# A limit of 8 blocks on how far ahead weight halves are split

## The chip, the cores and the metric

The kernel runs on one core of a Trainium2 chip. The metric is the device time of one execution in microseconds (us), the median of several runs. TensorE (PE) multiplies matrices, VectorE (DVE) and ScalarE (ACT) work element by element, GpSimd (POOL) likewise, and the queue of SyncE (SPq) issues the transfers of weights from HBM. Each of these works through its own instructions in the order in which the program lists them.

## The reference

Two decoder layers in float32 for 256 tokens of width 1024:

```python
# layer 0: attention (8 stick-breaking heads, 8 latent heads), then a dense SwiGLU, hidden width 3584
h = _attention_layer(h, ...)
h = x + (silu(xn @ w_gate) * (xn @ w_up)) @ w_down
# layer 1: a state-space layer with GLU, then a SwiGLU with 8 experts, two for each token
h = _s5_layer(h, ...)
logits = xt @ w_router
top_vals, top_idx = lax.top_k(logits, 2)
gates = softmax(top_vals)
out[t] = sum over the two experts e of t: gate * ((silu(xt @ w_gate[e]) * (xt @ w_up[e])) @ w_down[e])
```

The expert stage reads all 8 experts, each with three matrices of 1024 x 3584, and is the larger part of the kernel's time.

## The kernel before

All weights pass through one stream of blocks, which `all_blocks` lists in the order of use. A block is 128 partitions by 2048 float32, 1 MB (1.0486 million bytes). `fetch` issues the transfer of the next block of the stream on SPq whenever a raw buffer is free in the program's order (`fill`, `drop`), and counts it in `nload`. Five raw buffers exist from the start; others come in as the earlier layers give up memory (`ex`, `ey`, `we0`, `tm`, `rot`, `wy0`, the pair `gx0`/`gx1`, `xl`, a pair from the ring of split halves, `sa`), so in the expert stage there are 15.

A product in float32 is made from three products in a faster format: a value w is split into wh and wl = w - wh, and `mm3` multiplies wh with the other side's high and low parts, and wl with its high part. Weights are split half a block at a time by `half`: ScalarE copies the half to wh (L228) and VectorE subtracts to get wl (L229). After the second half of a block its raw buffer is given back, and the next transfer of the stream is issued for it; that transfer waits until the split has read the buffer. The split halves stand in a ring, of six pairs first and five in the expert stage.

`take` hands out the next split half. Before that it splits halves ahead, up to `self.ahead` of them beyond the one in use (5, and 4 in the expert stage), as long as their blocks have been issued:

```python
while len(self.pairs) < min(i + ahead + 1, self.nsplit) and self.loaded:
    self.half()
```

The expert stage works on chunks (e, f): expert e, and 512 of the 3584 hidden columns. A chunk has four blocks of gate and up weights and two of down weights. Experts 0, 2, 4 and 6 in this order are wide (128 token places, split weights, three products each); experts 1, 3, 5 and 7 are narrow (64 places): their weights are multiplied as they come, in float32, and are not split. Their raw blocks lie in a list of their own (`whole`) and are given back when their products are done. `count` orders the experts by how many tokens they have, so that those with more become wide.

`MIXED` is the order of the chunks. It begins with three or four wide chunks, then alternates narrow and wide ones, and ends each pair of experts with narrow chunks alone. For experts 2 and 3, and the start of expert 4:

```
(2,0) (2,1) (2,2) (3,0) (2,3) (3,1) (2,4) (3,2) (2,5) (3,3) (2,6) (3,4) (3,5) (3,6) (4,0) ...
```

`ffn` runs the chunks in this order, and the down product of a chunk comes after the gate and up products of the next one; `ffn_order` lists the blocks accordingly, four of gate and up, then the two of down of the chunk before. So the down blocks of (2,6) stand behind the gate and up blocks of (3,4), and after them come 12 narrow blocks before those of (4,0). With experts 0 and 1 it is 18 narrow blocks between the down blocks of (0,6) and the first of (2,0).

When a wide expert's last down product is done, its rows are scaled into Y on ScalarE (L1672) and VectorE (L1673), in two halves n = 0 and 1, each as soon as its part is done and the one before it is used. The products that put Y back in the order of tokens (`scatter`, L1681 and L1682) are listed within the following narrow chunks (`hook`, `step`), and so is the gathering of the next wide expert's tokens (`prep`, L1620). L724 and L758 are the narrow chunks' products, L257 to L259 those of `mm3`; L742 turns a narrow chunk's hidden values, L1727 the selection of a wide expert's tokens.

Of the kernel before, what the change touches and what calls it, by code (L numbers as in the profile page):

```python
# [147 lines left out]
class Net:  # L148
# [19 lines left out]
    def plan(self, blocks):  # L168


        self.blocks, self.nload, self.loaded, self.plain, self.pairs, self.used = blocks, 0, [], {}, [], 0
        self.whole = []
        self.nsplit = 2 * sum(not isinstance(b, tuple) or len(b) == 3 for b in blocks)
        self.fill()

    def fetch(self, buf, keep=True):


        if self.nload == len(self.blocks):
            if keep:  # L180
                self.free.append(buf)
            return
        src = self.blocks[self.nload]
        self.nload += 1
        src, *how = src if isinstance(src, tuple) else (src,)
        src = src() if callable(src) else src
        n = src.shape[-1]
        if isinstance(buf[0], tuple):
            w = [p.tile([P, 1024], F32, tag=t, name="raw")[:, :n // 2] for p, t in buf]
            for x in range(2):  # L190
                self.nc.sync.dma_start(w[x], src[:, n // 2 * x:n // 2 * (x + 1)])
        else:
            w = buf[0].tile([P, 2048], F32, tag=buf[1], name="raw")[:, :n]
            self.nc.sync.dma_start(w, src)
            if len(how) != 1:
                w = [w[:, :n // 2], w[:, n // 2:]]
        if how == [None]:
            w = w if isinstance(w, list) else [w[:, :n // 2], w[:, n // 2:]]
            self.whole.append(([a[:, 512 * x:512 * x + 512] for a in w for x in range(2)], buf if keep else None))
        elif len(how) == 1:  # L200
            self.plain[how[0]] = (w, buf if keep else None)
        else:
            self.loaded.append((w, buf if keep else None, how))

    def fill(self):
        while self.free and self.nload < len(self.blocks):
# [6 lines left out]

    def half(self, sub=None):

        ws, buf, gain = self.loaded[0]
        x = self.second
        w = ws[x]
        pr = self.ring.pop(0)
        self.ring.append(pr)  # L220
        wh, wl = (pool.tile([P, 1024], F32R, tag=tag, name="w" + nm)[:, :w.shape[-1]] for (pool, tag), nm in zip(pr, "hl"))
        if gain:
            for j in range(2):
                c, g = slice(512 * j, 512 * j + 512), self.gain(gain[0], gain[1] + j + 2 * x)
                self.nc.scalar.activation(wh[:, c], w[:, c], AF.Copy, scale=g)
                self.nc.vector.scalar_tensor_tensor(out=wl[:, c], in0=w[:, c], scalar=g, in1=wh[:, c].bitcast(F32), op0=ALU.mult, op1=ALU.subtract)
        else:
            self.nc.scalar.copy(wh, w)  # L228
            (sub or self.sub).tensor_tensor(out=wl, in0=w, in1=wh.bitcast(F32), op=ALU.subtract)  # L229
        self.pairs.append((wh, wl))  # L230
        self.second ^= 1
        if x:
            self.loaded.pop(0)
            self.drop(buf)
# [5 lines left out]
    def take(self, kk, ahead=None):  # L240


        i = self.used
        ahead = self.ahead if ahead is None else ahead
        while len(self.pairs) < min(i + ahead + 1, self.nsplit) and self.loaded:
            self.half()
        self.used += 1
        n = self.pairs[i][0].shape[-1] // kk
        return [tuple(t[:, j * n:j * n + n] for t in self.pairs[i]) for j in range(kk)]
# [118 lines left out]
    def attention(self, kp):  # L368
# [4 lines left out]
        with ExitStack() as st:  # L373
# [266 lines left out]
            def out(n, half):  # L640
                W = self.takek(4, 0)
                for b in range(2):
                    if half == 0:
                        pw[n, b] = bank([P, 512])
                    for kk in range(4):
                        k = 4 * half + kk
                        self.mm3(pw[n, b], mh[:, k, blk[b]], ml[:, k, blk[b]], *W[kk], k == 0, k == KD - 1)
# [1180 lines left out]
```

## Time and profile before

| | us |
|---|---|
| median of 3 runs | 1317.21 (1316.95 to 1317.34) |
| the profiled execution | 1316.26 |
| its span, first to last instruction | 1313.3 |
| TensorE busy | 1271.5 (97%) |
| VectorE busy | 831.7 (63%) |
| ScalarE busy | 635.8 (48%) |
| transfers, mean over the span | 321 GB/s |

The profile names a group of instructions by the line of the kernel, the engine, the operation and the tiles it writes and reads. Busy time of TensorE is modelled: products are pipelined, each is shown with its whole latency, so that busy is not the same as working at peak rate. An idle time ahead of an instruction is shown in brackets with what ended it. In the tables of windows each row gives the window, its length, the busy time of PE, PEld (weight loads), DVE, ACT and POOL with the number of instructions, then the granted clock of TensorE as a share of full speed, the busy share of the 16 DMA engines, and GB/s.

### The profile page before, as it was taken

The page shows a single profiled execution, that of the slowest core. Times are in us where ns is not written, and L with a number is a line of the kernel's source. Part 1 is how long each engine was busy: PE and PEld are TensorE (multiplying, and loading weights), DVE is VectorE, ACT ScalarE, POOL GpSimd, SP SyncE. Part 2 cuts the span into 40 slices and gives each one's busy share as a digit, 9 for nine tenths or more (in the row PEclk, how much of TensorE's full clock was granted, in tenths as well). Part 3 has the DMA queues.
Part 4 walks back from the last instruction along what each step waited for, and adds up shares of the span by engine and source line. Part 5 has one row for each costly group of instructions (what it writes and reads, how often), then busy time and mean ns, then how long its engine had stood idle before and what let it go on. Part 6 is the DMA issues. An engine that isn't in the chain of part 4 may idle for free.

```text
span 1313.3 us, 18300 instructions
## 1 busy us (share of the span) xinstructions
PE 1271.5 (97%) x6782; PEld 905.1 (69%) x6782; DVE 831.7 (63%) x1114; ACT 635.8 (48%) x833; POOL 177.9 (14%) x284
## 2 busy tenths in 40 slices
PE   8999999999998999999999999799999989999997
PEld 8867999999997777664567665457655645756652
DVE  6877868567876897652377565248755525855642
ACT  6665444444444676551366554236644425645530
POOL 2842993013611000000000000000000000000000
PEclk9999999999999899999999999899999989999999
DMA  8505654545437699999999999999999999899991
GB/s 315 214 1 199 235 191 140 211 167 189 166 128 300 226 349 364 419 418 418 418 417 417 420 418 418 381 415 375 384 419 417 418 373 420 336 405 416 419 418 72
DMA packets 66368, 421.21 MB, mean 321 GB/s; under 512 B 7504, under 2 KB 8784, under 8 KB 21472
## 3 DMA queue, kind: packets, MB, share of 16 engines
q1 hardware_dynamic: 65088, 418.15, 80.4%
q10 hardware_dynamic: 1008, 1.27, 0.3%
q8 instruction: 55, 0.90, 0.3%
q0 software_dynamic: 176, 0.56, 0.1%
q14 instruction: 41, 0.34, 0.1%
HBM read 418.89 MB, written 1.05 MB: 320 GB/s over the span
## 4 chain that ended last, share of the span: by engine, by line


## 5 line engine op out<-in xcount | busy, mean ns | idle before, releaser
L229 DVE TENSOR_TENSOR wl<-raw,wh 128x1024 fp32r<-128x1024 f32 (+1 forms) x456 | 549.3, 1236 | 155.7 <-ACT wh L228 139.1
L228 ACT CAST wh<-raw 128x1024 fp32r<-128x1024 f32 (+1 forms) x456 | 468.3, 1045 | 187.2 <-PE dn L259 57.9
L724 PE MATMUL pgu<-raw,we 128*64 128x512 f32 x896 | 203.7, 596 | 0.0
L257 PE MATMUL pgu<-wh,wy 128*128 128x512 f32 x448 | 178.2, 398 | 0.0
L258 PE MATMUL pgu<-wl,wy 128*128 128x512 f32 x448 | 174.7, 390 | 0.8 <-DVE wl L229 0.8
L259 PE MATMUL pgu<-wh,wy 128*128 128x512 f32 x448 | 174.5, 390 | 0.0
L724 PEld LDWEIGHTS pgu<-raw,we 128*64 128x64 f32 x896 | 61.1, 137 | 115.4 <-issue 113.4
L257 PE MATMUL pgu<-dxh,wh 128*128 128x256 f32 x448 | 127.3, 284 | 0.5 <-DVE h L686 0.5
L259 PE MATMUL pgu<-dxh,wl 128*128 128x256 f32 x448 | 126.8, 283 | 0.0
L258 PE MATMUL pgu<-dxl,wh 128*128 128x256 f32 x448 | 126.7, 283 | 0.0
L257 PE MATMUL dn<-wh,gh 128*128 128x512 f32 x280 | 112.0, 400 | 0.0
L258 PE MATMUL dn<-wl,gh 128*128 128x512 f32 x280 | 109.4, 391 | 0.0
L259 PE MATMUL dn<-wh,gl 128*128 128x512 f32 x280 | 109.3, 390 | 0.0
L758 PE MATMUL dn<-raw,gh 128*64 128x512 f32 x448 | 101.9, 597 | 0.5 <-ACT gh L744 0.5
L257 PEld LDWEIGHTS pgu<-wh,wy 128*128 128x128 f32 x448 | 84.1, 188 | 22.6 <-issue 4.1
L259 PEld LDWEIGHTS pgu<-wh,wy 128*128 128x128 f32 x448 | 84.1, 188 | 17.9
L258 PEld LDWEIGHTS pgu<-wl,wy 128*128 128x128 f32 x448 | 84.2, 188 | 17.5 <-DVE wl L229 1.2
L797 DVE TENSOR_TENSOR gl<-pgt,gh 128x512 fp32r<-128x512 f32 x27 | 18.7, 692 | 114.3 <-ACT gh L796 113.4
L257 PEld LDWEIGHTS pgu<-dxh,wh 128*128 128x128 f32 x448 | 85.9, 192 | 1.1 <-DVE h L686 0.7
L258 PEld LDWEIGHTS pgu<-dxl,wh 128*128 128x128 f32 x448 | 86.0, 192 | 0.3
L259 PEld LDWEIGHTS pgu<-dxh,wl 128*128 128x128 f32 x448 | 85.9, 192 | 0.0
L796 ACT CAST gh<-pgt 128x512 fp32r<-128x512 f32 x27 | 15.8, 585 | 143.3 <-PE pgt L790 143.3
(445 smaller groups left out, 1566.0 us busy)
## 6 DMA issues: line engine op xcount, KB each, us to landing
raw<-in_wm_dram SPq DMA_DIRECT2D x292, 1024.0 KB, 10.3
raw<-in_wm_dram SPq DMA_DIRECT2D x88, 512.0 KB, 10.6
raw<-in_wd_dram SPq DMA_DIRECT2D x42, 1024.0 KB, 4.9
raw<-in_wqkv_dram SPq DMA_DIRECT2D x6, 1024.0 KB, 6.1
raw<-in_wo_dram SPq DMA_DIRECT2D x4, 1024.0 KB, 5.9
raw<-in_wglu_dram SPq DMA_DIRECT2D x4, 1024.0 KB, 4.9
raw<-in_ws_dram SPq DMA_DIRECT2D x2, 1024.0 KB, 4.9
raw<-in_wc_dram SPq DMA_DIRECT2D x4, 416.0 KB, 6.7
```

The costliest lines, as they stand in the source:

```text
L228: self.nc.scalar.copy(wh, w)
L229: (sub or self.sub).tensor_tensor(out=wl, in0=w, in1=wh.bitcast(F32), op=ALU.subtract)
L257: mm(out, sh, mh, start=start, stop=False)
L258: mm(out, sh, ml, start=False, stop=False)
L259: mm(out, sl, mh, start=False, stop=stop)
L724: nc.tensor.matmul(pg[64 * j:64 * j + 64], x(k), W[j][0][k % 4], start=(k == 0), stop=(k == KD - 1))
L758: nc.tensor.matmul(job["acc"][64 * n:64 * n + 64], gts[0][:, k], W[n][0][k], start=(f == 0 and k == 0), stop=(f == NF - 1 and k == 3))
L796: nc.scalar.copy(gh, a)
L797: v.tensor_tensor(out=gl, in0=a, in1=gh.bitcast(F32), op=ALU.subtract)
```

## The change

Each block remembers its place in the stream (`nload` when it was issued) beside its data, and each split half remembers its block's place in a list `at`. `take` splits a half ahead only if its block lies at most 8 places behind the block of the half now in use. The half that is needed itself is always split.

```diff
@@ plan
-        self.blocks, self.nload, self.loaded, self.plain, self.pairs, self.used = blocks, 0, [], {}, [], 0
+        self.blocks, self.nload, self.loaded, self.plain, self.pairs, self.used, self.at = blocks, 0, [], {}, [], 0, []
@@ fetch
-            self.loaded.append((w, buf if keep else None, how))
+            self.loaded.append((w, buf if keep else None, how, self.nload))
@@ half
-        ws, buf, gain = self.loaded[0]
+        ws, buf, gain, at = self.loaded[0]
...
         self.pairs.append((wh, wl))
+        self.at.append(at)
@@ take
-        while len(self.pairs) < min(i + ahead + 1, self.nsplit) and self.loaded:
+        while len(self.pairs) < min(i + ahead + 1, self.nsplit) and self.loaded and (len(self.pairs) <= i or self.loaded[0][3] - self.at[i] <= 8):
             self.half()
```

## The prediction

> **What bounds the kernel now.** I read the page first (engine shares, slices), then the list of waits, then the windows of 25 us, and, where a window fell out of line, the order of time on ScalarE (ACT), TensorE (PE) and the DMA queue (SPq). From the page:
>
> ```profile
> span 1313.3 us, 18300 instructions
> PE 1271.5 (97%) x6782; PEld 905.1 (69%) x6782; DVE 831.7 (63%) x1114; ACT 635.8 (48%) x833; POOL 177.9 (14%) x284
> ...
> PEclk9999999999999899999999999899999989999999
> DMA  8505654545437699999999999999999999899991
> ```
>
> TensorE is busy for 97% of the span, and from slice 15 to slice 39 (the expert stage) the DMA engines are busy nearly as fully. Each slice is 32.8 us. The granted clock dips in slices 26 and 33, about 820 to 853 us and 1050 to 1083 us, and DMA in slice 35. The list of waits has a row for it:
>
> ```profile
> ACT wh L228 <- DMA raw<-in_wm_dram: 24.6, 2, 13.3
> ```
>
> Twice, 24.6 us in all, a ScalarE copy of a weight half (`half`, L228) stands at the head of its queue until a transfer lands. In order of time on ScalarE, start and duration first, the idle time ahead of it in brackets:
>
> ```profile
> 840.97 1.99 ACT L228 CAST wh<-raw 128x1024 fp32r<-128x1024 f32 x2 [13.28 <-DMA raw<-in_wm_dram]
> 842.86 0.68 ACT L1672 ACTIVATE Y<-dn,gs 128x512 fp32r<-128x512 f32 x1
> 843.51 1.99 ACT L228 CAST wh<-raw 128x1024 fp32r<-128x1024 f32 x2
> ...
> 1060.48 1.99 ACT L228 CAST wh<-raw 128x1024 fp32r<-128x1024 f32 x2 [11.32 <-DMA raw<-in_wm_dram]
> ```
>
> Two halves wait, then the Y of a finished expert (L1672) runs, then two more halves. The Y stands behind halves that it has nothing to do with, and TensorE needs it:
>
> ```profile
> 837.09 0.46 PE L742 MATMUL pgt<-cst,sg 64*128 64x64 f32 x4
> 843.60 0.79 PE L1681 MATMUL px<-Y,ST 128*128 128x512 f32 x1 [6.04 <-ACT Y L1672]
> ...
> 846.57 3.39 PE L1620 MATMUL px<-S,xn 128*128 128x128 f32 x16
> 849.89 3.65 PE L724 MATMUL pgu<-raw,we 128*64 128x512 f32 x16
> ...
> 860.73 0.50 PE L1681 MATMUL dn<-Y,ST 128*128 128x512 f32 x1
> ...
> 862.25 2.05 PE L1620 MATMUL dn<-S,xn 128*128 128x128 f32 x16 [0.31 <-DVE h L1216]
> 864.24 3.65 PE L724 MATMUL pgu<-raw,we 128*64 128x512 f32 x16
> ...
> 1058.57 0.46 PE L742 MATMUL pgt<-cst,sg 64*128 64x64 f32 x4
> 1063.11 0.79 PE L1681 MATMUL dn<-Y,ST 128*128 128x512 f32 x1 [4.08 <-ACT Y L1672]
> ...
> 1071.21 3.75 PE L724 MATMUL pgu<-raw,we 128*64 128x512 f32 x16
> ```
>
> TensorE idles 6.04 and 4.08 us, and its next twenty products run slowly: 16 products of L1620 take 3.39 us at 846.57 and 2.05 us at 862.25.
>
> **What the change refuses.** I count in the stream of 336 expert blocks that `moe_blocks` lists, with the four halves ahead that `self.ahead = 4` allows. Within wide chunks, and where wide and narrow chunks alternate, the farthest half lies 8 blocks on (four or six narrow blocks between), which the limit still lets through. Only where the last two or three narrow chunks stand alone (12 or 18 blocks) does it lie farther: from the down blocks of (2,6), places 152 and 153, to (4,0) at 166 and 167, which is 13 or 14; the same from (4,6) to (6,0); and 19 or 20 from (0,6) to (2,0). The layers ahead keep within 8, as 5 halves ahead are at most 3 weight blocks and two small plain ones. Fifteen raw buffers are in turn by then: with 152 and 153 split and given back they hold 154 to 168, so (4,0), and likewise (6,0), has been issued when the half is asked for, while 64 to 78 do not reach (2,0) at 82. So eight halves move, four at each of two places, from ahead of the last narrow chunks to the start of the next wide expert. Nothing is added or removed: 8 copies (L228), 8 subtractions (L229), and four block transfers issued later on SPq.
>
> **What the two stalls cost.** First place: 6.04 idle; then from L1681 to L724 849.89 - 843.60 = 6.29 us, where the same run undisturbed takes 864.24 - 860.73 = 3.51, so 2.78 more; together 8.82. Second: 4.08 idle, and 1071.21 - 1063.11 = 8.10 against 3.51, so 4.59 more; together 8.67. Sum 17.5. With the copies gone from the queue, Y is made when (2,6)'s down product ends, before the narrow half that fills TensorE up to 837.55, so I take the whole of it.
>
> A second way of reckoning uses the place at which nothing was split ahead, (0,6) to (2,0), and with it the cost of the moved work:
>
> ```profile
> 625.75 0.46 PE L742 MATMUL pgt<-cst,sg 64*128 64x64 f32 x4
> ...
> 645.95 3.60 PE L758 MATMUL dn<-raw,gh 128*64 128x512 f32 x16
> 649.49 0.50 PE L257 MATMUL pgu<-wh,wy 128*128 128x512 f32 x1
> ...
> 674.88 0.44 PE L1727 MATMUL dn<-cst,S 128*128 128x128 f32 x2 [0.77 <-DVE h L1216]
> ...
> 871.25 0.50 PE L257 MATMUL pgu<-wh,wy 128*128 128x512 f32 x1
> ...
> 896.40 0.44 PE L1727 MATMUL px<-cst,S 128*128 128x128 f32 x2
> ...
> 1092.09 0.50 PE L257 MATMUL pgu<-wh,wy 128*128 128x512 f32 x1
> ...
> 1117.46 0.44 PE L1727 MATMUL dn<-cst,S 128*128 128x128 f32 x2 [0.78 <-DVE h L1216]
> ```
>
> From the turn of the last chunk but one (L742) to the first wide product it is 649.49 - 625.75 = 23.74 us there, and 871.25 - 837.09 = 34.16 at the first stall, which holds one scatter of Y more (862.25 - 860.73 = 1.52): 8.90 too long, beside the 8.82 above.
>
> **What the moved halves cost.** After the change, (4,0) and (6,0) begin as (2,0) does now:
>
> ```profile
> 646.69 6.92 ACT L228 CAST wh<-raw 128x1024 fp32r<-128x1024 f32 x7
> ```
>
> ```profile
> 647.75 9.17 DVE L229 TENSOR_TENSOR wl<-raw,wh 128x1024 fp32r<-128x1024 f32 x8 [0.24 <-ACT wh L228]
> ```
>
> The halves start on ScalarE while TensorE is still in the last narrow down products (L758 at 645.95), and the first wide product follows at 649.49 with no idle time. This cover is 3.54 us against about 2.1 for the first half (6.92/7 = 0.99 and 9.17/8 = 1.15); without it each start would come 2.1 later. After that a half is needed every 1.4 us (six products at the rate of 16 in 3.65) and made every 1.15. From the first wide product to the L1727 behind the first two chunks it takes 25.39 us at (2,0), 25.15 at (4,0), 25.37 at (6,0): the crowd costs 0.24 and 0.02. I take 0.3 for both. Ends: nothing (it cannot gain, as TensorE does not idle at 871.25), and four halves bare at each place, 8 x 1.15 = 9.2. I take the near end because (2,0) is the same code in the same state.
>
> **The DMA queue.** Windows, of which the last two figures are the DMA share and GB/s, and the queue's own order of time:
>
> ```profile
> 550.00:575.00 25.00, 25.00 (x115) 14.62 (x114) 13.98 (x13) 11.48 (x14) 0.00 (x0) 1.00 1.01 417
> 840.00:850.00 10.00, 5.67 (x22) 4.76 (x24) 7.14 (x8) 5.50 (x8) 0.00 (x0) 0.52 0.78 297
> 900.00:935.00 35.00, 35.00 (x160) 23.57 (x159) 25.18 (x23) 21.09 (x24) 0.00 (x0) 1.00 0.93 346
> 1060.00:1085.00 25.00, 19.94 (x92) 10.93 (x92) 9.82 (x12) 6.96 (x10) 0.00 (x0) 0.80 0.94 361
> 1120.00:1155.00 35.00, 35.00 (x161) 24.20 (x161) 26.11 (x24) 21.77 (x24) 0.00 (x0) 1.00 0.90 328
> 1285.00:1305.00 20.00, 18.99 (x94) 6.85 (x92) 2.72 (x5) 1.71 (x4) 0.00 (x0) 1.00 0.00 1
> ```
>
> ```profile
> 827.58 1.34 SPq L191 DMA_DIRECT2D raw<-in_wm_dram  x2
> 844.43 13.49 SPq L194 DMA_DIRECT2D raw<-in_wm_dram  x8
> ```
>
> SPq issues nothing from 828.9 to 844.4: its next transfer waits for a late half, and buffers that narrow chunks give back at 837 stand behind it. Against 417 GB/s, DMA loses 10 x 120/417 = 2.9 us at the first stall and 25 x 56/417 = 3.4 at the second; the change gives these back. It loses 35 x 71/417 = 6.0 and 35 x 89/417 = 7.5 us more in the wide stretches, where TensorE is full (35.00) and buffers are the limit. So TensorE can run 17.2 us sooner and DMA follow within 19.8. The held buffers (two blocks until the wide start) delay transfers by at most 2 x 2.51 us (1.0486 MB at 417) at each place, hidden as long as blocks lie ready: (4,0)'s first block landed at 841.0 and will be wanted at 871.25 - 8.8 = 862.4, 8 blocks ahead. At the end, transfers stop by 1285, and TensorE works on to 1305.
>
> **Sum.** 17.5 - 0.3 = 17.2 us. The profiled execution took 1316.26 us (span 1313.3 and 2.96 around it), 0.95 below the median 1317.21. It should become 1299.1, and the median 1300.0.
>
> **Rivals.**
> (a) DMA is the bound, and stalls of engines only let it catch up. Only its own 2.9 + 3.4 = 6.3 come back: 1310.9. For it: 417 GB/s through most of the stage. Against: blocks ready 8 ahead, and no wait of TensorE on an expert block among the longest waits. [...]
> (b) The moved halves stand bare: 17.5 - 9.2 = 8.3, so 1308.9. Against: the start at 649.49.
> (c) The limit refuses nothing that waited: 1317.2. It would be so if the halves at 840.97 lay within 8 blocks. Their order, two halves, Y, two halves, fits (2,6)'s down takes alone.
> (d) Slower: blocks are not ready, so the stalls were free, and the two held buffers cost 2 x 5.0 us: 1327.2. It decides once a narrow product waits for its raw block, that is, once the 8 blocks in hand are gone.
>
> On the clock: the row is 0.52 over 840 to 850. [...]
>
> **How the numbers follow.** Forecast 0.74; (a) 0.09, (b) 0.05, (c) 0.07, (d) 0.05. No change means within 0.2% (2.6 us), about what a measurement of this kernel can tell. Faster: 0.74 + 0.09 + 0.05 = 0.88; same 0.07; slower 0.05. Low end: 17.5 gained, no cost, the two waits on VectorE ahead of L1727 gone too (0.77 + 0.78), and 0.95 for profile against median: 1297.2. High end: through (b) to (a), 1310.9; 0.12 is left out.
>
> **What would show it.** Right: no ScalarE wait on a raw transfer above 1 us; L1681 straight behind L742 at about 837.5; clock 1.00 over 800 to 1080; L228 in a run of seven or eight at (4,0) and (6,0), with the first wide product near 862 and 1075; DMA at 417 through 840 to 850; more idle DMA nowhere. Wrong: a new wait ahead of the first wide L257, or L724 and L758 waiting for raw.

## The result and the profile after

| | before, us | after, us |
|---|---|---|
| median | 1317.08 (1316.87 to 1317.34, 4 runs) | 1298.01 (1297.70 to 1298.15, 4 runs) |
| the profiled execution | 1316.26 | 1297.99 |
| its span | 1313.3 | 1295.9 |

The ratio is 0.9855, with a 95% interval of 0.9838 to 0.9872: 19.1 us by the medians, where 17.2 were forecast. From the page of the changed kernel, the rows that answer to those shown of before:

```profile
span 1295.9 us, 18302 instructions
...
PEclk9999999999999899999999999999999999999999
DMA  8605654554447689999999999999999999999991
```

The two dips of the clock in slices 26 and 33 are gone, and so is the one of DMA in slice 35. In the order of time on ScalarE, Y now stands at the head of the queue, and the halves of (4,0) and (6,0) come in runs of seven at their start (the lines behind L230 have moved by one: L1672 is now L1673, L742 is L743, L257 to L259 are L258 to L260; in kernels with more lines added they have moved further):

```profile
831.76 0.69 ACT L1673 ACTIVATE Y<-dn,gs 128x512 fp32r<-128x512 f32 x1 [3.21 <-PE dn L260]
...
859.84 6.95 ACT L228 CAST wh<-raw 128x1024 fp32r<-128x1024 f32 x7
```

And on TensorE, first and second place:

```profile
837.96 0.46 PE L743 MATMUL pgt<-cst,sg 64*128 64x64 f32 x4
838.35 0.50 PE L1682 MATMUL px<-Y,ST 128*128 128x512 f32 x1
...
841.27 3.65 PE L725 MATMUL pgu<-raw,we 128*64 128x512 f32 x16
...
851.73 0.46 PE L743 MATMUL pgt<-cst,sg 64*128 64x64 f32 x4
...
859.10 3.60 PE L759 MATMUL dn<-raw,gh 128*64 128x512 f32 x16
862.64 0.50 PE L258 MATMUL pgu<-wh,wy 128*128 128x512 f32 x1
...
1049.98 0.46 PE L743 MATMUL pgt<-cst,sg 64*128 64x64 f32 x4
1050.37 0.50 PE L1682 MATMUL dn<-Y,ST 128*128 128x512 f32 x1
...
1053.87 3.65 PE L725 MATMUL pgu<-raw,we 128*64 128x512 f32 x16
...
1064.33 0.46 PE L743 MATMUL pgt<-cst,sg 64*128 64x64 f32 x4
...
1074.65 0.50 PE L258 MATMUL pgu<-wh,wy 128*128 128x512 f32 x1
```

L1682, the scatter that needs Y, follows L743 without idle time (0.39 us later; before, 6.51), and the first wide product follows the narrow down products at 862.64 without idle time. The turns of narrow chunks that end the two places in the profile of before (each row's window ends within the group, so it counts two and three of its four products; the start is what is read):

```profile
860.34 0.34 PE L742 MATMUL pgt<-cst,sg 64*128 64x64 f32 x2
...
1081.76 0.40 PE L742 MATMUL pgt<-cst,sg 64*128 64x64 f32 x3
```

From turn to turn it took 860.34 - 837.09 = 23.25 us and now takes 851.73 - 837.96 = 13.77: 9.48 less. At the second place it was 1081.76 - 1058.57 = 23.19 and is 1064.33 - 1049.98 = 14.35: 8.84 less. I set such intervals, from one turn of hidden values (L743, L791) to the next, of both traces side by side through the whole expert stage. There are 54; 51 agree within 0.03 us. Two of the others are the stalls. The third is 1.60 longer after, at the start of expert 2, and is a matter of the clock (below). So -9.48 - 8.84 + 1.60 = -16.7, and 0.7 that the changed kernel's execution was ahead when the expert stage began: together the 17.4 of the spans.

The windows, with clock, DMA share and GB/s at the end:

```profile
840.00:850.00 10.00, 10.00 (x55) 4.15 (x55) 2.46 (x4) 1.46 (x3) 0.00 (x0) 1.00 1.02 419
900.00:935.00 35.00, 35.00 (x161) 24.92 (x160) 25.75 (x24) 22.71 (x25) 0.00 (x0) 1.00 1.01 405
1050.00:1075.00 25.00, 24.69 (x132) 11.65 (x131) 8.08 (x11) 6.84 (x11) 0.00 (x0) 1.00 1.02 418
1120.00:1155.00 35.00, 35.00 (x158) 24.55 (x157) 24.87 (x23) 23.28 (x26) 0.00 (x0) 1.00 1.01 406
```

TensorE is full, or nearly so, where it was idle, and DMA moves 419 and 418 GB/s where it moved 297 and 361. It also moves 405 and 406 in the wide stretches, where it had fallen to 346 and 328. The work there now comes about 9 and 18 us sooner; in windows moved by as much it moves 404 and 405. What the transfer queue waits for in these stretches, in both kernels, is buffers that splits and products give back: in 900 to 935 of before it stands 28.1 us for the subtractions L229 and 5.2 for the products L724, in the changed kernel 19.5 and 5.2. I infer that TensorE's lead, which frees buffers sooner, has filled the gaps of before.

### The profile page after: what moved, and what is told of

It reads as the page before. It is cut to its first block, busy times and chain, and to the rows that moved or that the text cites. A ratio compares the mean times of both kernels' runs of the same rounds, so it can differ in the third digit from the quotient of the medians.

```text
span 1295.9 us, 18302 instructions
## 1 busy us (share of the span) xinstructions
PE 1266.7 (98%) x6782; PEld 901.7 (70%) x6782; DVE 831.5 (64%) x1114; ACT 635.6 (49%) x833; POOL 177.7 (14%) x284
## 4 chain that ended last, share of the span: by engine, by line
## 5 line engine op out<-in xcount | busy, mean ns | idle before, releaser
L229 DVE TENSOR_TENSOR wl<-raw,wh 128x1024 fp32r<-128x1024 f32 (+1 forms) x456 | 548.7, 1236 | 123.2 <-ACT wh L228 107.4
L258 PE MATMUL pgu<-wh,wy 128*128 128x512 f32 x448 | 178.8, 399 | 0.0
L259 PE MATMUL pgu<-wl,wy 128*128 128x512 f32 x448 | 175.5, 392 | 0.8 <-DVE wl L229 0.8
L260 PE MATMUL pgu<-wh,wy 128*128 128x512 f32 x448 | 175.0, 391 | 0.0
L258 PE MATMUL pgu<-dxh,wh 128*128 128x256 f32 x448 | 127.3, 284 | 0.5 <-DVE h L687 0.5
L260 PE MATMUL pgu<-dxh,wl 128*128 128x256 f32 x448 | 126.8, 283 | 0.0
L259 PE MATMUL pgu<-dxl,wh 128*128 128x256 f32 x448 | 126.8, 283 | 0.0
L258 PE MATMUL dn<-wh,gh 128*128 128x512 f32 x280 | 112.0, 400 | 0.0
L259 PE MATMUL dn<-wl,gh 128*128 128x512 f32 x280 | 109.4, 391 | 0.0
L260 PE MATMUL dn<-wh,gl 128*128 128x512 f32 x280 | 109.3, 390 | 0.0
L759 PE MATMUL dn<-raw,gh 128*64 128x512 f32 x448 | 101.9, 597 | 0.5 <-ACT gh L745 0.5
L258 PEld LDWEIGHTS pgu<-wh,wy 128*128 128x128 f32 x448 | 84.4, 188 | 22.8 <-ACT wh L228 2.4
L260 PEld LDWEIGHTS pgu<-wh,wy 128*128 128x128 f32 x448 | 84.5, 189 | 18.0
L259 PEld LDWEIGHTS pgu<-wl,wy 128*128 128x128 f32 x448 | 84.5, 189 | 17.6 <-DVE wl L229 1.2
L258 PEld LDWEIGHTS pgu<-dxh,wh 128*128 128x128 f32 x448 | 86.0, 192 | 1.1 <-DVE h L687 0.7
L259 PEld LDWEIGHTS pgu<-dxl,wh 128*128 128x128 f32 x448 | 86.0, 192 | 0.3
L260 PEld LDWEIGHTS pgu<-dxh,wl 128*128 128x128 f32 x448 | 85.9, 192 | 0.0
```

The lines of the kernel that those rows point to most:

```text
L258: mm(out, sh, mh, start=start, stop=False)
L259: mm(out, sh, ml, start=False, stop=False)
L260: mm(out, sl, mh, start=False, stop=stop)
L759: nc.tensor.matmul(job["acc"][64 * n:64 * n + 64], gts[0][:, k], W[n][0][k], start=(f == 0 and k == 0), stop=(f == NF - 1 and k == 3))
```

## The experiments

Two theories. **Y**: the copies of far halves stand at the head of ScalarE's queue until their transfer lands, and Y, which TensorE needs next, stands behind them. **T**: what counts is the transfer queue; the late splits hold back transfers, narrow buffers pile up behind them, and DMA pauses. A third, **A**, is that any stand of ScalarE costs about its length. The first four runs share their runs of before (median 1316.40 us), the last four theirs (1317.02).

**Buffers kept, halves early** (held_buffers). Halves are split ahead as before the change, but the raw buffers of the far ones are given back when the block is in use:

```diff
+            if far:
+                self.held.append((at, buf))
+            else:
+                self.drop(buf)
...
-        while ... and (len(self.pairs) <= i or self.loaded[0][3] - self.at[i] <= 8):
-            self.half()
+        while len(self.pairs) < min(i + ahead + 1, self.nsplit) and self.loaded:
+            self.half(far=len(self.pairs) > i and self.loaded[0][3] - self.at[i] > 8)
+        while self.held and self.held[0][0] <= self.at[i]:
+            self.drop(self.held.pop(0)[1])
```

> All four halves at each place are split ahead on ScalarE and VectorE as before the change, but their raw buffers are given back only when the block is in use, so that the narrow chunks' buffers pass them on the transfer queue. Theory Y: no gain, 1316 to 1317.5 us, TensorE idle 6 and 4 us as before, although DMA no longer pauses around 845. Rival T: the gain of the change, 1298 to 1302 us.

Measured 1315.64 us, ratio 0.9995 (0.9985 to 1.0004). Its ScalarE, transfer queue and TensorE, in order of time:

```profile
838.96 1.99 ACT L228 CAST wh<-raw 128x1024 fp32r<-128x1024 f32 x2 [13.55 <-DMA raw<-in_wm_dram]
```

```profile
834.91 23.32 SPq L194 DMA_DIRECT2D raw<-in_wm_dram  x7
```

```profile
841.59 0.79 PE L1687 MATMUL px<-Y,ST 128*128 128x512 f32 x1 [6.31 <-ACT Y L1678]
```

The queue now issues at 834.91, as soon as the first narrow blocks come free and 6.7 us ahead of the scatter, and DMA moves 415 and 414 GB/s in 835 to 840 and 840 to 845. TensorE idles 6.31 us all the same. In before, too, DMA still moved 419 in 835 to 840, when TensorE already stood (from 837.55). So T is refuted as the cause of this stall. One part of the expectation missed: the pause of DMA is not gone but comes later. After two transfers the queue issues nothing until 851.04, and DMA falls to 111 and 195 GB/s in 845 to 850 and 850 to 855. The second place is 1.73 us longer than before.

**Far halves on GpSimd** (far_on_gpsimd). All halves are split ahead as before, and the transfers wait as before, but the far halves are copied and subtracted on the idle GpSimd:

```diff
+        elif far:
+            self.nc.gpsimd.tensor_copy(wh, w)
+            self.nc.gpsimd.tensor_tensor(out=wl, in0=w, in1=wh.bitcast(F32), op=ALU.subtract)
         else:
             self.nc.scalar.copy(wh, w)
...
+            self.half(far=len(self.pairs) > i and self.loaded[0][3] - self.at[i] > 8)
```

> All four halves at each place are split ahead as before the change, but those that lie more than 8 places on are copied and subtracted on GpSimd, so that ScalarE and VectorE do not wait; the transfers behind them on the transfer queue wait as before. Theory Y: 1297.5 to 1300 us, GpSimd waiting about 12 us on the raw transfer at each place, DMA share again below 0.9 in some 10 us there. Rival T: no gain, 1314 to 1317 us.

Measured 1303.36 us, ratio 0.9898 (0.9882 to 0.9915), between the two. From turn to turn both places are 9.49 and 8.84 shorter than before, so both stalls are gone, as Y has it. But GpSimd gets to the first half at 840.58 and the transfer queue issues nothing until 847.50:

```profile
847.50 11.27 SPq L194 DMA_DIRECT2D raw<-in_wm_dram  x9
```

```profile
825.00:850.00 25.00, 25.00 (x128) 13.09 (x126) 6.02 (x11) 3.83 (x7) 9.18 (x6) 1.00 0.82 330
850.00:875.00 25.00, 24.69 (x120) 14.86 (x118) 11.44 (x12) 10.60 (x13) 4.24 (x3) 1.00 0.86 350
1050.00:1075.00 25.00, 24.69 (x131) 11.39 (x129) 7.23 (x10) 4.72 (x8) 12.62 (x8) 1.00 0.77 305
1075.00:1100.00 25.00, 23.63 (x106) 15.72 (x104) 15.55 (x16) 14.71 (x17) 1.70 (x1) 1.00 0.90 361
1175.00:1200.00 25.00, 23.37 (x107) 13.20 (x106) 12.12 (x12) 10.49 (x13) 0.00 (x0) 1.00 1.01 418
```

Against 418 GB/s, DMA loses 25 x (88 + 68 + 113 + 57)/418 = 19.5 us in these four windows, and in the last pair of experts TensorE loses time at full DMA rate: 23.37 of 25 us busy, and from turn to turn 6.3 us more than before in all (0.33, 1.10, 1.70, 1.78, 1.38). It is ScalarE's copies (L231 in this kernel) that wait for raw blocks there, 35.8 us in 16 waits, where the changed kernel has one of 0.3 us; TensorE stands behind them by way of VectorE. So about 13 us of lost DMA time seem to have been borne, and the rest came back as waits. What the transfer queue holds back is no part of the two stalls, but is paid once the blocks in hand are gone. These waits more than account for the 3.4 us by which the time lies above the range of Y.

**Two halves ahead of Y, or behind it** (two_before_y, limit13). The same two halves, the first block of (4,0) and of (6,0), are split early, once at the takes of the first down block, ahead of the first Y, and once at those of the second, behind it (limit 13):

```diff
-... self.loaded[0][3] - self.at[i] <= 8):
+... self.loaded[0][3] - self.at[i] <= 8 or (self.loaded[0][3] - self.at[i] == 14 and self.at[i + 2] - self.at[i] == 1)):   # two_before_y
+... self.loaded[0][3] - self.at[i] <= 13):                                                                                # limit13
```

> Only the two halves of the first block of (4,0), and of (6,0), are split early, at the takes of the first down block, so that they stand ahead of the first Y (n = 0) on ScalarE, as before the change; the other two halves at each place come late. Theory Y (the stall costs because Y, which TensorE needs next, stands behind copies that wait for a transfer): both stalls return in full, as Y ran at 842.86 behind the first two halves; 1316 to 1317 us, ScalarE waits of 11 to 14 us on a raw transfer, TensorE idle about 6 and 4 us ahead of the first scatter. Rival T (what counts is how many transfers stand behind late splits on the transfer queue): one block held instead of two, so about half, 1306 to 1309 us.

> The limit is 13 places instead of 8: the same two halves are split early at each place, but at the takes of the second down block, so that they stand behind the first Y (n = 0) and ahead of the second. The ScalarE wait on the transfer stays, 8 to 11 us long. Theory Y: TensorE hardly waits, since the next things of ScalarE that it needs are the turned hidden values at about 844.8 and the second Y at 852, and the transfer lands near 841; 1297.5 to 1300 us. Rival A (any stand of ScalarE for a far transfer costs about its length): 1305 to 1315 us. Rival T (the transfer queue): like two_before_y, 1306 to 1309 us.

Measured 1312.68 us (ratio 0.9966, 0.9954 to 0.9978) and 1304.13 us (0.9906, 0.9887 to 0.9925). In two_before_y both stalls return but for 1.17 and 1.20 us; T's half gain is excluded, though Y's number was 3 us too high. In limit13 the first place is 9.48 shorter than before, as with the change, though ScalarE stands until the transfer lands, as in before (9.83 us instead of 13.28, since Y now runs first):

```profile
829.80 0.69 ACT L1673 ACTIVATE Y<-dn,gs 128x512 fp32r<-128x512 f32 x1 [3.21 <-PE dn L260]
840.31 1.99 ACT L228 CAST wh<-raw 128x1024 fp32r<-128x1024 f32 x2 [9.83 <-DMA raw<-in_wm_dram]
```

```profile
836.38 0.50 PE L1682 MATMUL px<-Y,ST 128*128 128x512 f32 x1
```

TensorE goes on at 836.38, in the middle of ScalarE's 9.83 us. So A is refuted at this place: the stand cost nothing, as nothing behind it was wanted. But the second place is only 1.04 shorter, and here neither Y nor my number for it held: 7.8 us are lost. Its rows, VectorE first, then TensorE:

```profile
1053.03 2.55 DVE L229 TENSOR_TENSOR wl<-raw,wh 128x1024 fp32r<-128x1024 f32 x2 [9.73 <-ACT wh L228]
1055.50 0.68 DVE L1217 TENSOR_TENSOR h<-h,dn 128x512 f32<-128x512 f32 x1
```

```profile
1056.24 3.56 PE L1621 MATMUL dn<-S,xn 128*128 128x128 f32 x16 [6.62 <-DVE h L1217]
```

Y itself came in time, and the scatter ran. But the subtraction L229 of the same half stands at the head of VectorE's queue, with the addition h behind it that empties the scatter's PSUM bank `dn`, and L1621 wants that bank. At the first place L1621 had gone to a `px` tile, which comes from a pool of four, and waited for nothing. The theory has to be wider than Y: a far half blocks ScalarE and, through wl, VectorE, and the price is set by the first thing behind it, on either, that TensorE wants. At the second place Y was the wait that TensorE met in before, but putting Y ahead of the copies is not enough there.

**The changed kernel again** (after_again), beside the next three:

> The changed kernel itself, unaltered, on the chip of the runs beside it, so that they can be set against it. All theories: 1297 to 1299.5 us. Place by place the same as in its first profile, except for a dip of the clock of about 1.5 us near 675 to 695 us that some executions show and others do not.

Measured 1296.94 us (1295.79 to 1297.93), ratio 0.9843 (0.9827 to 0.9860). Its intervals agree with the first profile's throughout, with the 1.57 us near 675 in the profiled execution.

**A limit of 3** (limit3), so that down blocks are not split across narrow ones either:

> The limit is 3 places, so that in the alternating stretches too no half of a wide chunk's down blocks is split across the narrow blocks ahead of it. At 19 places (4 for the first pair of experts, 5 for each other) the first half is then copied only when the narrow chunk's gate is done, and TensorE, which goes straight from the narrow gate and up products to the wide down product, should idle for the copy and part of the subtraction. Theory Y, with the cover that the change counts on: (4,0) and (6,0) cost nothing because a narrow down product of 3.5 us lies ahead of them, and these 19 have no such cover: 1.7 to 2.9 us each, so 1330 to 1355 us. Rival (splitting late costs nothing anywhere, the engines have room): 1297 to 1301 us.

Measured 1369.84 us, ratio 1.0398 (1.0381 to 1.0416). The list of waits, and two of the places in order of time on TensorE:

```profile
PE dn L258 <- ACT wh L228: 29.4, 19, 1.7
PE dn L259 <- DVE wl L229: 14.4, 19, 0.8
```

```profile
519.32 0.50 PE L258 MATMUL dn<-wh,gh 128*128 128x512 f32 x1 [1.65 <-ACT wh L228]
520.58 0.50 PE L259 MATMUL dn<-wl,gh 128*128 128x512 f32 x1 [0.76 <-DVE wl L229]
...
552.04 0.50 PE L258 MATMUL dn<-wh,gh 128*128 128x512 f32 x1 [1.65 <-ACT wh L228]
```

```profile
520.00:525.00 5.00, 4.42 (x12) 3.53 (x13) 5.00 (x6) 4.03 (x6) 0.00 (x0) 0.66 0.95 319
550.00:555.00 5.00, 2.59 (x10) 1.61 (x9) 3.67 (x4) 4.54 (x6) 0.00 (x0) 1.00 1.01 424
```

At 19 places, as counted, and (29.4 + 14.4)/19 = 2.3 us of idle time at each in the mean, within the 1.7 to 2.9. The total missed, since an interval from turn to turn with such a place grew by 1.86 to 2.80 us where the clock held (550 to 555) and by 4.35 to 4.39 where it fell (0.66 in 520 to 525), and since the starts of experts 2, 4 and 6 grew too, by 3 to 5 us, which I had not counted; TensorE waits there for VectorE (L1662, 7.5 us in 3 waits, 2.6 in the changed kernel), and the rest of that growth stays open. The direction stands: a late half without cover costs. In the same run the interval that holds the first products of (4,0), with L759 ahead of them, takes 16.62 us against 16.60 before, and that of (6,0) 16.01 against 16.00, so the late halves are free there.

**12 and 9 raw buffers** (buffers12, buffers9). `sa`, `rot` and `tm` are not given back, and for 9 also not `wy0`, the `gx` pair and `xl`.

> The changed kernel with 12 raw buffers in the expert stage instead of 15 (tm, rot and sa are not given back). Then (4,0) and (6,0) are never issued when the down blocks ahead are used, so the limit refuses nothing. If TensorE is the bound and blocks lie ready with 10 us or more in hand: 1297.5 to 1301 us. Rival (a), the transfers set the time: three blocks less in hand cost about 3 x 2.5 us or more: 1305 to 1315 us.

> The same with 9 raw buffers (wy0, the gx pair and xl are kept back as well): six blocks, 15 us of transfer, less in hand. If the reserve is about 13 us, as the run with the far halves on GpSimd suggests (19 us of DMA lost, 6 us of waits on raw blocks), TensorE now waits on raw blocks late in each pair of experts: 1302 to 1325 us, with DMA near 417 GB/s ahead of those waits. If the reserve is still not used up: 1298 to 1301 us.

Measured 1297.28 us (1295.41 to 1298.17), ratio 0.9851 (0.9835 to 0.9867): the time of the changed kernel. By the places in the stream the limit refuses nothing here, as (4,0) is not issued when it would be asked for: the kernel before the change with 12 buffers would do the same work in the same order. That kernel was not run. With 9 it is 1339.57 us, ratio 1.0184 (1.0158 to 1.0211). The waits of ScalarE on raw blocks, with 12 and with 9:

```profile
ACT wh L228 <- DMA raw<-in_wm_dram: 22.0, 24, 3.5
```

```profile
ACT wh L228 <- DMA raw<-in_wm_dram: 105.6, 34, 9.2
```

With 12 there are 24 short waits (0.9 us in the mean), which no interval on TensorE shows. With 9 the intervals late in each pair of experts are longer by up to 4.4 us, and the kernel loses 42.6 us against the run with 15, more than I had allowed (1325): with too few blocks in hand, long waits of ScalarE come back all over the stage. So the changed kernel can spare 3 blocks but not 6 (7.5 and 15 us of transfer), in line with the 13 us above.

## Why the prediction was right

**The mechanism.** At the first place it is as forecast: the far copies stood ahead of Y, and with Y first (limit13) or the copies elsewhere (far_on_gpsimd) the stall is gone. At the second place the prediction had only half of it. Y did stand behind the copies, but VectorE's subtraction of the same halves blocked a PSUM bank as well (6.62 us of idle TensorE at 1056.24), and in limit13, with Y out of the way, only 1.04 of the 8.84 us came back. The forecast did not suffer, since the change takes the copies and the subtractions away together.

**The stalls.** Forecast 8.82 and 8.67, measured 9.48 and 8.84. The step that undersized the first is the undisturbed run of 3.51 us, taken from 860.73: it holds a wait of 0.31 us on VectorE for a PSUM bank. Now that nothing is late, the first place takes 841.27 - 838.35 = 2.92 us. That is 0.6 of the 0.7 us missed; the second place has the wait (1053.87 - 1050.37 in the changed trace is 3.50) and was sized right within 0.2.

**The moved halves.** Forecast 0.3 for both, measured nothing: the intervals behind 862.64 and 1074.65 agree with before within 0.02 us, and there is no idle time ahead of them. I had read the 0.24 between (2,0) and (4,0) as the price of the crowd, but at (4,0) the stretch is as long with the crowd as it was without. The cover of 3.5 us, called the reason, is borne out by limit3: the late halves cost 2.3 us of idle time where it is absent, and nothing at (4,0) and (6,0), where it is there.

**DMA.** Both terms came as forecast: the pauses at the stalls are gone, and the DMA time lost in the wide stretches, counted by GB/s, fell from 6.0 and 7.5 us to about 1 each (35 x 12/417 and 35 x 11/417). The busy share there is 1.01, so what is left is a lower rate and not idle time. The lead of 18.3 us was followed: the queue issues its last block of weights at about 1252.8 us instead of 1269.9. There is little to spare, about 2 us of lost time and the blocks in hand. The prediction reckoned with 8 of these; the runs with fewer buffers show between 3 and 6 that can be spared. A change that saves more than that on TensorE should meet rival (a); no run here tries it. Whether DMA could move more than the 418 GB/s that it moves over most of the stage (417 to 419, at a busy share of 1.01 or 1.02), none shows either. The time fell by three times the 6.3 us of that rival, because the kernel before had lost 19.8 us of DMA time.

**Rivals.** (a) and (b) were excluded by the time, (c) by the trace, (d) by the blocks in hand. The condition of (d), that these run out, can be met: with 9 buffers the changed kernel is slower than the kernel before with 15, though it is ScalarE's copies and not narrow products that wait for raw blocks. That the two held buffers alone cost anything is not shown.

**Size.** 1300.0 was forecast and 1298.0 measured. Of the 2.0, 0.8 are in the two stalls, 0.3 in the moved halves, and 0.9 lies between executions: the forecast kept the gap of 0.95 between profile and median, but the profiled execution of after is at its median. That the two profiled executions differ by 18.3, just what the two stalls come to, is luck: that of after lost 1.6 us to the clock, was 0.7 ahead when the expert stage began, and took 0.9 less outside its span, and these cancel.

## What to carry to other kernels

Work that is pulled ahead stands in the same queues as work that is due: here Y ran at 842.86, behind two halves that had stood 13.28 us, and at 831.76 in the changed kernel. Look how far ahead in the stream of transfers it reaches, not how many items, and ask of every engine it touches what stands behind it and when that is wanted: in one kernel (limit13) the same wait of nearly 10 us cost nothing at one place and 7.8 us at the other, by whether TensorE next wanted something that stood behind it. What was moved late was free behind 3.5 us of cover and cost 2.3 us of idle time without it, and with six blocks fewer in hand the kernel lost 42.6 us, so count both the cover and the blocks.

## What the runs showed of the hardware

Much of the difference between profiles outside the two places is whether the clock falls at a short idle time. In both profiles there are two short waits of TensorE near 672 us at the start of expert 2. Before and after, in windows of 5 us:

```profile
675.00:680.00 5.00, 5.00 (x24) 4.13 (x25) 5.00 (x11) 2.62 (x3) 0.00 (x0) 1.00 1.01 406
```

```profile
675.00:680.00 5.00, 5.00 (x17) 3.93 (x17) 3.75 (x9) 2.07 (x2) 0.00 (x0) 0.71 1.03 415
```

The waits are 0.94 and 0.77 us before, 0.93 and 0.78 after; the clock is 1.00 once and 0.71 the other time, and the interval 1.60 us longer. Both profiles of the changed kernel and that of far_on_gpsimd have this dip; those of before, limit13, held_buffers, buffers12 and buffers9 do not. That suggests that it goes with the execution and not with what a kernel changes. limit3 shows the same within one execution: at 17 of its 19 places the two waits are the same (1.65 and 0.76 us), and behind them seven or eight products take 0.63 us instead of 0.39 at 6 places (among them the one with the clock of 0.66 in 520 to 525), and none does at the other 11 (among them the one with 1.00 in 550 to 555). So the clock fell, at some executions and places and not at others, behind 1.7 us of idle time in two pieces, and in limit3 behind 2.4 us.
